# Branch prefetch hints placed inside the last second matmul of a ReGLU MLP kernel, and none on SyncE

## The chip, the cores and the metric

The kernel runs on one core of a Trainium2 chip. Times are device microseconds (us) of an execution. The profile's span, from the first to the last instruction, is about 1.8 us shorter than that time.

## The reference

```python
# x (16, 256, 512), w1 (512, 4096), w2 (2048, 512), all float32
h = x @ w1
gate, value = np.split(h, 2, axis=-1)
h = np.maximum(gate, 0) * value
return (h @ w2).astype(np.float32)
```

## The kernel before

The kernel has a fast way in float16, with fewer products per block than the plain method, and a general way for inputs whose sizes do not fit. While the last second matmul runs, the fast way judges statistics of the inputs and writes a flag. Every engine loads that flag into a register and branches (in the kernel before, 488 to 695 ns for the load and 45 to 496 ns for the branch). With the inputs used here the branch is always taken, over the whole body of the general way, to the end of the program.

```python
def tile_reglu_mlp_kernel(ctx, tc, x, w1, w2, out):
    ...                                             # cut
    with ExitStack() as fast:
        unfit = fast_way(fast, tc, x2, w1, w2, out2, flag)
    with tc.If(unfit > 0, label="general"):
        with ExitStack() as general:
            general_way(general, tc, x2, w1, w2, out2)
```

The fast way is written under a "manual schedule": each engine's instructions keep the order in which they were traced. The second matmul is a stream of 112 steps of four matmuls, and jobs are hung on its steps:

```python
    ctx.enter_context(tc.manual_schedule(engines={ENG.PE, ENG.DVE, ENG.Activation, ENG.Pool, ENG.SP}))
    ...                                             # cut
            job(18, lambda: verdict.append(judge()))
            job(46, lambda: count(verdict[0]))
            job(78, lambda: verdict.append(nc.values_load(flag[0:1, 0:1], ...)))      # cut
            job(84, lambda: tc.mark_branch_hint_location("general", "LikelyTaken", [ENG.PE, ENG.DVE, ENG.SP]))
            advance(stream, 112, jobs)
```

A branch prefetch hint is an instruction of its own, BRANCH_PREFETCH_HINT in the traces (50 ns on PE, 51 on VectorE and 56 on SyncE in the kernel before), that is marked for a later branch; what it does at that branch is what the runs below measure. The last job asks for it at step 84. But in the built program the hints of PE (TensorE), VectorE (DVE) and SyncE (SP) stand as the first instruction of each engine, about 300 us ahead of the branch. The last outputs go out as three 128 KB transfers, one after another, from SyncE, each behind the copy that made its tile.

## Time and profile before

| | before |
|---|---|
| time, median of the first 3 runs | 308.57 us (308.36 to 308.63) |
| span of the profile | 307.2 us |
| PE busy | 301.6 us, 98% |
| end of the last ScalarE copy | 303.45 us |
| last output: issue, landing | 303.48, 306.19 us |

From the page of the kernel before (busy us, share of the span, x instructions; then the chain that ended last, by engine):

```profile
PE 301.6 (98%) x1905; PEld 184.2 (60%) x1905; DVE 236.0 (77%) x388; ACT 176.3 (57%) x348; POOL 151.2 (49%) x189
...
q8 instruction: 16, 0.26, 0.4%
q14 instruction: 12, 0.10, 0.1%
...
PE 96%; DMA 2%; SPq 1%; issue 0%; ACT 0%
```

PE bounds the kernel. The two lines of queues (packets, MB, share) are the instruction fetches. q8 carries 16 KB packets and is put down to PE: it has 17 in the three runs where PE's branch took over 4 us (e1, e3, e9), 16 in all others with a branch and 15 without one (e11). q14 carries 8 KB packets and is put down to the other engines: it has one more where VectorE's hint does not act (13 in e5, 14 in e6).

The start of the chain in order of time (start, length, what), of the kernel before:

```profile
0.68 0.06 issue
0.74 0.06 SPq L785
0.80 0.06 issue
0.85 0.40 SPq L488
...
2.79 5.41 DMA x_A<-in_x_dram
```

L785 is SyncE's hint (all end-of-program and hint instructions bear that line). It stands between the start barrier and the first load of x, and a tile of x is what PE waits for until 8.2 us.

The branches, in the view of source line L42 (duration minimum/median/maximum in ns, then first and last start in us), of the kernel before:

```profile
L42 PEldq COMPARE_BRANCH  x1: 496/496/496, 301.9 to 301.9; - x1
L42 DVEq COMPARE_BRANCH  x1: 90/90/90, 302.2 to 302.2; - x1
L42 DVEq EVENT_SEMAPHORE  x1: 21/21/21, 302.8 to 302.8; - x1
L42 PEldq EVENT_SEMAPHORE  x1: 51/51/51, 303.1 to 303.1; - x1
...
L42 SPq COMPARE_BRANCH  x1: 68/68/68, 304.9 to 304.9; - x1
```

The event semaphore of each engine is the first instruction at the branch's target.

### The profile page before, as it was taken

What the parts mean: (1) busy time and instruction counts of PE and PEld (TensorE: products, weight loads), DVE (VectorE), ACT (ScalarE), POOL (GpSimd) and SP (SyncE); (2) the same over time, 40 slices, a digit from 0 to 9 for tenths busy, and PEclk for the clock granted to TensorE, in tenths of its full rate; (3) what the DMA queues carried; (4) which work ended last, traced back from release to release, by engine and by line L of the source; (5) the groups of instructions that cost most, each with busy time, mean ns of one, the idle gap of its engine ahead of it and who ended that gap; (6) DMA issues with size and microseconds to landing.
All of it is one profiled execution on the core that took longest, in us unless ns stands there. A gap on an engine that the chain in (4) does not pass through costs nothing.

```text
span 307.2 us, 5283 instructions
## 1 busy us (share of the span) xinstructions
PE 301.6 (98%) x1905; PEld 184.2 (60%) x1905; DVE 236.0 (77%) x388; ACT 176.3 (57%) x348; POOL 151.2 (49%) x189
## 2 busy tenths in 40 slices
PE   8999999999999999999999999999999999999994
PEld 7744444588844444478864444458884444447883
DVE  2579888899778888887538888888536888888851
ACT  2488896455865555537855555546866555553231
POOL 2389999800068999300029889700007988700000
PEclk9999999999999999999999999999999999999999
DMA  6985779965775270001354910000325110001132
GB/s 204 358 259 179 239 171 176 229 123 80 260 209 88 69 137 3 0 0 55 136 182 108 207 34 2 0 2 9 130 101 174 35 34 0 3 1 34 54 106 87
DMA packets 35836, 32.87 MB, mean 107 GB/s; under 512 B 14432, under 2 KB 31328, under 8 KB 35680
## 3 DMA queue, kind: packets, MB, share of 16 engines
q1 hardware_dynamic: 33536, 26.22, 28.3%
q0 software_dynamic: 2272, 6.29, 11.4%
q8 instruction: 16, 0.26, 0.4%
q14 instruction: 12, 0.10, 0.1%
HBM read 27.26 MB, written 12.58 MB: 130 GB/s over the span
## 4 chain that ended last, share of the span: by engine, by line
PE 96%; DMA 2%; SPq 1%; issue 0%; ACT 0%
PE Y L250 26%; PE X L250 17%; PE W L250 17%; PE Y L362 14%; PE W L362 9%; PE X L362 9%; DMA x_A<-in_x_dram 2%; PE X L325 1%; PE W L325 1%; PE Y L325 1%; PE Y L498 0%; PE X L498 0%; SPq L217 0%; SPq L488 0%; ACT o L405 0%
## 5 line engine op out<-in xcount | busy, mean ns | idle before, releaser
L250 PEld LDWEIGHTS <-w_T 128*128 128x128 f16 x496 | 48.3, 98 | 57.3 <-POOL w_T L232 1.1
L179 POOL TENSOR_TENSOR fold<-xh 128x1024 f32<-128x1024 f16 x16 | 30.3, 1894 | 94.6 <-DMA xh<-x 93.7
L250 PE MATMUL X<-x_A,w_B 128*128 128x512 f16 x248 | 73.8, 379 | 0.0
L250 PE MATMUL Y<-x_S,w_T 128*128 128x512 f16 x220 | 65.5, 379 | 0.0
L250 PEld LDWEIGHTS <-w_B 128*128 128x128 f16 x372 | 36.3, 98 | 42.1
L277 DVE SCALAR_TENSOR_TENSOR cc<-W,pu 128x512 f32<-128x512 f32 x62 | 42.9, 691 | 21.1 <-ACT pu L271 21.1
L257 ACT COPY Y<-X 128x512 f32<-128x512 f32 x62 | 35.4, 571 | 38.2 <-PE X L250 37.9
L271 ACT ACTIVATE pu<-Y 128x512 f32<-128x512 f32 x62 | 37.1, 598 | 33.9 <-PE Y L250 33.0
L182 POOL TENSOR_TENSOR fold<-fold 128x512 f32<-128x512 f32 (+2 forms) x96 | 51.8, 539 | 7.5
L362 PEld LDWEIGHTS <-w_stage 128*128 128x128 f16 x512 | 50.0, 98 | 5.9
L287 DVE SCALAR_TENSOR_TENSOR cc<-Y,pu 128x512 f32<-128x512 f32 x62 | 42.9, 691 | 6.7
L282 DVE SCALAR_TENSOR_TENSOR g<-X,cc 128x512 f16<-128x512 f32 x62 | 42.8, 691 | 2.3
L299 DVE SCALAR_TENSOR_TENSOR g<-Y,cc 128x512 f16<-128x512 f32 x62 | 42.2, 681 | 1.8 <-PE Y L250 1.8
L362 PEld LDWEIGHTS <-g 128*128 128x128 f16 x384 | 37.5, 98 | 8.2
L264 ACT ACTIVATE pu<-W 128x512 f32<-128x512 f32 x62 | 37.2, 600 | 0.8 <-PE W L250 0.6
L250 PE MATMUL W<-x_S,w_B 128*128 128x512 f16 x124 | 36.9, 379 | 0.0
L250 PE MATMUL W<-x_S,w_T 128*128 128x512 f16 x124 | 36.9, 379 | 0.0
L250 PE MATMUL Y<-x_A,w_T 128*128 128x512 f16 x124 | 36.9, 379 | 0.0
L362 PE MATMUL X<-w,g 128*128 128x256 f16 x256 | 31.9, 273 | 0.0
L394 DVE SCALAR_TENSOR_TENSOR o<-W,pu 128x256 f32<-128x256 f32 x16 | 6.8, 423 | 19.4 <-PE W L362 19.4
L169 DVE TENSOR_TENSOR w_stage<-g 128x1024 f16<-128x1024 f16 x32 | 21.4, 684 | 0.2
L232 POOL TENSOR_TENSOR w_T<-w_stage 128x512 f16<-128x512 f32 (+1 forms) x16 | 18.7, 1173 | 2.5 <-DMA w_stage<-in_w_dram 2.5
(100 smaller groups left out, 307.5 us busy)
## 6 DMA issues: line engine op xcount, KB each, us to landing
w_stage<-in_w_dram SPq DMA_DIRECT2D x14, 512.0 KB, 6.0
out_dram<-o SPq DMA_DIRECT2D x26, 256.0 KB, 2.1
x<-in_x_dram POOLq DMA_DIRECT2D x4, 1024.0 KB, 9.1
xh<-x SPq DMA_DIRECT2D x16, 256.0 KB, 3.0
w<-in_w_dram POOLq DMA_DIRECT2D x2, 1024.0 KB, 10.2
out_dram<-o SPq DMA_DIRECT2D x12, 128.0 KB, 1.7
w_stage<-in_w_dram SPq DMA_DIRECT2D x4, 256.0 KB, 5.4
x_S<-in_x_dram SPq DMA_DIRECT2D x4, 256.0 KB, 6.5
```

The costliest lines, as they stand in the source:

```text
L169: eng.tensor_tensor(o[n], o[i0], o[i1], op=op)
L179: nc.gpsimd.tensor_tensor(fold, t, t, op=MULT)
L182: nc.gpsimd.tensor_tensor(fold[:, :, :m], fold[:, :, :m], fold[:, :, m:2 * m], op=ADD)
L250: nc.tensor.matmul(ps, wop[wn][:, b, self.jb * P:(self.jb + 1) * P], self.xo[xn][:, b, :], start=fresh and b == 0, stop=b == 1, skip_group ...
L257: nc.scalar.copy(out=self.Y, in_=self.X)
L264: nc.scalar.activation(self.p5, self.W, COPY, scale=GS)
L271: nc.scalar.activation(self.u2, self.Y, COPY, scale=GS)
L277: nc.vector.scalar_tensor_tensor(out=self.c12, in0=self.W, scalar=GS, in1=self.u2, op0=MULT, op1=ADD)
L282: nc.vector.scalar_tensor_tensor(out=self.g[:, self.jb, :TH], in0=self.X, scalar=0.0, in1=self.c12, op0=MAX, op1=MULT)
L287: nc.vector.scalar_tensor_tensor(out=self.c22, in0=self.Y, scalar=GS, in1=self.p5, op0=MULT, op1=ADD)
L299: nc.vector.scalar_tensor_tensor(out=self.g[:, self.jb, TH:], in0=self.Y, scalar=0.0, in1=self.c22, op0=MAX, op1=MULT)
L362: nc.tensor.matmul(ps, self.op[an][:, i], vop[wn][:, i], start=name in ("P1", "P5") and i == 0, stop=i == NJ // 2 - 1, skip_group_check=True)
```

## The change

The intent is that the hint stands where it was asked for, near the branch, and that SyncE, whose program is short, has none. To pin the hint, the manual order is left, the hint is marked with a dependency on the engine's last traced instruction, and the manual order is entered again.

```diff
+    order = ctx.enter_context(ExitStack())
+    def in_order():
+        order.enter_context(tc.manual_schedule(engines={ENG.PE, ENG.DVE, ENG.Activation, ENG.Pool, ENG.SP}))
+    in_order()
...
+    def hint_here():
+        order.close()
+        traced = nc.cur_bb.bb.instructions
+        n = len(traced)
+        tc.mark_branch_hint_location("general", "LikelyTaken", [ENG.PE, ENG.DVE])
+        for i in nc.cur_bb.bb.instructions[n:]:
+            last = next(x for x in reversed(traced[:n]) if x.engine == i.engine and "Tile" not in type(x).__name__)
+            tc.add_manual_dep(i, last.name, ..., reason="the hint stays where it was traced")   # cut
+        in_order()
...
-            job(84, lambda: tc.mark_branch_hint_location("general", "LikelyTaken", [ENG.PE, ENG.DVE, ENG.SP]))
+            job(40, hint_here)
```

More of the change, by code (lines that the diff above doesn't have):

```diff
@@ L113, in fast_way @@
     NB = 2 * TH // P
-    ctx.enter_context(tc.manual_schedule(engines={ENG.PE, ENG.DVE, ENG.Activation, ENG.Pool, ENG.SP}))
+    order = ctx.enter_context(ExitStack())
+    def in_order():
+        order.enter_context(tc.manual_schedule(engines={ENG.PE, ENG.DVE, ENG.Activation, ENG.Pool, ENG.SP}))
+    in_order()
     wpool = ctx.enter_context(tc.tile_pool(name="wpool", bufs=1))
@@ L645, in judge @@
         return fit
+    def hint_here():
[5 more added lines that the diff above has]
+            last = next(x for x in reversed(traced[:n]) if x.engine == i.engine and "Tile" not in type(x).__name__)
+            tc.add_manual_dep(i, last.name, mybir.DependencyInfo(mybir.DependencyClass.NoSync, mybir.DependencyReason.DATA),
+                              reason="the hint stays where it was traced")
+        in_order()
     def count(fit):
```

## The prediction

> **What bounds the kernel now.** TensorE. The page gives PE 301.6 us busy of a 307.2 us span (98%), clock 0.999; the chain that ended last is 96% PE. The rest are two ends. At the start the chain runs through SyncE: its branch hint (0.74 to 0.80 us), its DMA issues from 0.85 us, then an x tile's landing until 8.2 us, which releases transposes. At the end, in the timeline: last matmul about 303.05, last ScalarE copy until 303.45, last output DMA issue until 304.8, its landing about 306.3, closing barrier until 307.2.
>
> **What the change does**, by the order of instructions on each engine:
> - SyncE loses its hint (56 ns, in the chain at 0.74 us).
> - PE and VectorE lose theirs at the start (50 and 51 ns, about 0.8 us). Neither is in the chain.
> - PE gets its hint in the last second matmul, just before product P5 of pair 1 (about 286.9 us); VectorE just before the flag's comparison (about 288.7 us).
> - A side effect: one VectorE sum (S1 of pair 2, 0.68 us) moves from just before the flag to inside the judgement, after its first comparison (284.2 us). ScalarE and GpSimd keep their order.
>
> **What it is worth.** The intent is a cheaper taken branch over the general body. The view of that source line shows the branches: PE's starts at 301.9 and takes 0.50 us, its next instruction is at 303.1; VectorE's starts at 302.2 (0.09 us), next at 302.8; SyncE's at 304.9 (0.07 us), next at 305.1. [...] But both reach the final barrier by about 303.2, while SyncE waits for the last output until 306.3: 3 us of slack. So a faster branch is worth no time. SyncE's branch also lies before the wait for the landing, and its gap of 0.1 us shows no fetch wait.
>
> On the critical path remain:
> - start: -0.06 us (without SyncE's hint every x load issues earlier).
> - PE's hint in a stream of matmuls 0.109 us apart: 0 to +0.05 us[...].
> - the moved sum delays the sums of pair 1 by 0.68 us. S1 of pair 1 would end at about 286.2, needed at 286.85; S2 at 286.9, needed at 287.7; the others have over 1 us. No new PE wait.
>
> Sum: about -0.03 us, below the spread of the three runs (308.36 to 308.63).
>
> **Predicted: 308.5 us, 308.1 to 308.9 in 8 of 10. Faster by over 2%: 0.01; within 2%: 0.98; slower by over 2%: 0.01.**
>
> **What would show each step.** First x issue at about 0.79 instead of 0.85 us; hints of about 50 ns at 287 and 289 us; PE's matmuls there still 0.109 us apart; PE's branch perhaps down from 0.50 to 0.1 us and its closing drain earlier, with the last landing and the end of the span unmoved; no PE wait for a sum at 286 to 290 us.
>
> **What would make it wrong.** [...] If the hint at the first instruction had disturbed fetching for the whole run, PE would gain, but at 98% busy there is little to gain. If the moved sum waits for PE, up to 1 us could be added.

## The result

| | before | after |
|---|---|---|
| time, median of 6 runs each | 308.54 us (308.28 to 308.84) | 308.24 us (307.99 to 308.39) |
| span of the profile | 307.2 us | 306.4 us |
| PE's branch | 496 ns | 496 ns |
| VectorE: end of branch to first instruction at its target | 0.54 us | 3.11 us |
| last output, issue to landing | 2.71 us | 2.60 us |

Ratio 0.9989, 95% interval 0.9976 to 1.0002. The change is within 2%, and a gain is not clear of noise by this pair alone.

The start of the chain after the change:

```profile
0.73 0.13 issue
0.86 0.28 DVE warm L149
1.15 0.05 issue
1.19 2.74 PE Y L153 x24
```

SyncE's first x issue, after:

```profile
0.74 0.87 SPq L493 DMA_DIRECT2D x_A<-in_x_dram  x2
```

It moved from 0.85 to 0.74 us, by 0.11 us: the hint and the gap behind it. In this run x landed early enough that PE never waited for it, and the chain begins at VectorE's memset instead. That memset too is earlier, from 0.95 to 0.86 us, because VectorE's hint is gone from in front of it.

The branches after the change:

```profile
L42 PEldq COMPARE_BRANCH  x1: 496/496/496, 301.3 to 301.3; - x1
L42 DVEq COMPARE_BRANCH  x1: 90/90/90, 301.6 to 301.6; - x1
L42 PEldq EVENT_SEMAPHORE  x1: 51/51/51, 302.5 to 302.5; - x1
...
L42 SPq COMPARE_BRANCH  x1: 53/53/53, 303.2 to 303.2; - x1
L42 DVEq EVENT_SEMAPHORE  x1: 21/21/21, 304.8 to 304.8; - x1
```

PE's branch is what it was. VectorE's has become 2.6 us worse, with a hint 15 us ahead of it. The instruction fetches after the change:

```profile
q8 instruction: 16, 0.26, 0.4%
q14 instruction: 14, 0.11, 0.1%
```

Of the two packets that q14 has more, only one belongs to VectorE's branch. The other, at 96.6 us, goes with SyncE: it stands in every trace without a hint on SyncE and is missing in the two with one (before and e12).

Matching PE's 1905 matmuls one by one, PE is 0.62 to 0.64 us earlier than before from 11 us on, and this lead changes by no more than 40 ns from one matmul to the next up to the end. So PE's late hint and the moved VectorE sum cost PE nothing, and all of the lead arises at the start. How far it is a property of the change, and not of that one run's loads, the experiments must tell.

### The profile page after: what moved, and what is told of

Read it like the earlier page. It is cut to its first block, busy times and chain, and to the rows that moved or that the text cites. A ratio compares the mean times of both kernels' runs of the same rounds, so it can differ in the third digit from the quotient of the medians.

```text
span 306.4 us, 5282 instructions
## 1 busy us (share of the span) xinstructions
PE 301.2 (98%) x1905; PEld 184.6 (60%) x1905; DVE 235.7 (77%) x388; ACT 176.4 (58%) x348; POOL 151.3 (49%) x189
## 3 DMA queue, kind: packets, MB, share of 16 engines
q0 software_dynamic: 2272, 6.29, 11.4%
## 4 chain that ended last, share of the span: by engine, by line
PE 98%; ACT 0%; DVE 0%; issue 0%
PE Y L255 26%; PE X L255 17%; PE W L255 17%; PE Y L367 14%; PE X L367 9%; PE W L367 9%; PE X L330 1%; PE Y L153 1%; PE W L330 1%; PE Y L503 1%; PE Y L330 1%; PE X L503 1%; PE Y L520 0%; PE Y L159 0%; PE Y L154 0%; ACT o L410 0%
```

## The experiments

Two questions came from the traces. Why did VectorE's branch lose 2.6 us with a hint closer to it, and does that matter? And where do the 0.3 us come from? Theory A: an engine keeps its hint until the branch, however early it was given, but the late hint on VectorE came too late for a fetch to be started. The rival B: hints do nothing, and 0.54 against 3.11 us is chance.

The first table gives, for every run, where the hints executed and what the branches did. The "fetch" is the engine's last instruction block fetch ahead of the branch, worked out from the times of the trace's instruction packets: 268 to 270 us on VectorE and 297.8 to 299.1 us on PE, except where noted.

| run | PE hint at | VectorE hint at | PE branch | VectorE gap | last output, issue to landing |
|---|---|---|---|---|---|
| before | 0.8 us | 0.8 us | 0.50 us | 0.54 us | 2.71 us |
| after | 285.2 | 286.5 | 0.50 | 3.11 | 2.60 |
| e1_no_hints | none | none | 4.48 | 3.03 | 3.94 |
| e2_no_sp | 0.8 | 0.8 | 0.50 | 0.54 | 2.46 |
| e3_moved_sum | none | none | 4.46 | 3.01 | 3.30 |
| e4_mid2 | 234.1 | 235.6 | 0.41 | 0.54 | 2.23 |
| e5_before_fetch | 264.2 | 265.7 | 0.41 | 0.54 | 2.35 |
| e6_after_fetch | 278.8 | 281.2 | 0.50 | 3.18 | 2.35 |
| e7_pe_just_ahead | 296.3 | 295.9 | 0.50 | 2.95 | 2.78 |
| e8_pe_just_behind | 298.0 (fetch at 299.9) | 296.0 | 0.66 | 3.07 | 2.98 |
| e9_pe_behind | 299.2 | 300.6 | 4.33 | 3.07 | 3.15 |
| e10_e8_again | 298.0 (fetch at 299.9) | 296.0 | 0.68 | 3.04 | 2.66 |
| e11_no_branch | no branch | no branch | none | none | 1.69 |
| e12_sp_hints_x8 | 0.8 | 0.8 | 0.50 | 0.54 | 2.62 |

The second table gives the times. Kernels of one group ran on the same chip in the same rounds.

| run | median us (range) | before, same rounds | ratio (95%) |
|---|---|---|---|
| e1_no_hints | 308.43 (307.52 to 310.36) | 308.28 | 0.9992 (0.9974 to 1.0010) |
| e2_no_sp | 308.20 (308.07 to 309.02) | 308.28 | 0.9991 (0.9978 to 1.0004) |
| e3_moved_sum | 308.93 (307.82 to 309.37) | 308.28 | 1.0008 (0.9992 to 1.0024) |
| e4_mid2 | 308.07 (307.82 to 308.51) | 308.28 | 0.9988 (0.9975 to 1.0000) |
| e5_before_fetch | 308.33, one run | 308.42 | - |
| e6_after_fetch | 308.06 (307.75 to 308.41) | 308.42 | 0.9996 (0.9979 to 1.0014) |
| e7_pe_just_ahead | 308.37 (307.82 to 308.57) | 308.42 | 0.9996 (0.9980 to 1.0012) |
| e8_pe_just_behind | 308.97 (308.65 to 309.08) | 308.42 | 1.0020 (1.0005 to 1.0035) |
| e9_pe_behind | 308.06 (307.63 to 308.84) | 308.45 | 0.9981 (0.9963 to 1.0000) |
| e10_e8_again | 308.88 (308.55 to 309.16) | 308.45 | 1.0010 (0.9989 to 1.0032) |
| e11_no_branch | 307.76 (307.44 to 308.17) | 308.45 | 0.9973 (0.9956 to 0.9991) |
| e12_sp_hints_x8 | 311.15 (310.64 to 311.46) | 308.45 | 1.0078 (1.0060 to 1.0096) |

All gave the right result. The kernel before itself ranged from 307.81 to 309.70 us in the last group, so differences of 0.3 us need care.

### e1_no_hints: no hint anywhere

```diff
-            job(84, lambda: tc.mark_branch_hint_location("general", "LikelyTaken", [ENG.PE, ENG.DVE, ENG.SP]))
```

> Kernel before with no hint on any engine. Theory A (the hint at the first instruction was kept until the branch, the late VectorE hint came too late to start a fetch): VectorE's gap after its branch is about 3.1 us as in the changed kernel, against 0.54 us before; if PE's hint also did something, PE's next instruction after its branch comes 1 us or more later than before's 1.2 us. Rival B (hints do nothing, 0.54 against 3.11 us is chance): VectorE's gap 0.5 us or anything. Time: if PE's branch also stalls by 3 us or more, PE ends after the last output's landing (2.7 us after the last ScalarE copy) and the time is 308.5 to 310 us; if only VectorE's stalls, 308.2 to 308.6 us. The start is as in the changed kernel: first x issue at about 0.8 us.

The branches without hints:

```profile
L42 PEldq COMPARE_BRANCH  x1: 4476/4476/4476, 302.1 to 302.1; - x1
L42 DVEq COMPARE_BRANCH  x1: 72/72/72, 302.4 to 302.4; - x1
L42 DVEq EVENT_SEMAPHORE  x1: 21/21/21, 305.5 to 305.5; - x1
L42 PEldq EVENT_SEMAPHORE  x1: 51/51/51, 306.6 to 306.6; - x1
```

Rival B falls. The hint at the first instruction, 301 us ahead of the branch, had worked all along on both engines: it spares PE about 4 us and VectorE 2.5 us at the branch. And VectorE's gap in the changed kernel is that of no hint at all. Yet PE was not the last engine even here. The last output landed at 307.62 us and PE drained at 306.77. The time did not settle what the miss costs: the six runs spread over 2.8 us.

### e2_no_sp: only SyncE's hint taken away

```diff
-..., [ENG.PE, ENG.DVE, ENG.SP]))
+..., [ENG.PE, ENG.DVE]))
```

> Kernel before, PE and VectorE hints at the first instruction kept, SyncE's hint left out. Theory A: VectorE's gap after its branch 0.54 us as before, PE as before. My account of the start: SyncE's first x issue 0.06 us earlier; time lower than before by 0.06 us. Rival C (the whole gain of 0.3 us comes through SyncE's hint): time lower by 0.3 us and PE's early lead of 0.2 to 0.64 us at 7.5 to 11 us seen again.

The first x issue came at 0.74 us, as after the change, and the branches are those of the kernel before. The ratio, 0.9991, is about that of the whole change (0.9989), but its interval includes both 0.06 and 0.3 us, so rival C was not excluded by the time. PE was 0.32 us behind the kernel before in this profile at 12 us, not ahead: the early lead is not seen again, and the profiles of single runs differ by more than the effect.

### e3_moved_sum: the changed kernel without its hints

```diff
-        tc.mark_branch_hint_location("general", "LikelyTaken", [ENG.PE, ENG.DVE])
```

> Changed kernel with its two late hints taken out: what remains is the moved VectorE sum and no hint anywhere. If the moved sum costs nothing: time equal to that of the kernel without hints within 0.15 us, PE's matmuls 0.109 us apart from 282 us on, no wait for a sum. If the late hints cost PE time, this is faster than the changed kernel by up to 0.05 us. If the late PE hint helps PE's branch, PE's next instruction after its branch comes 1 us or more later than the changed kernel's 1.2 us after the branch starts.

This keeps the one VectorE sum that leaving and re-entering the manual order had moved. From 11.4 us on, PE's matmuls keep a constant distance to the kernel before's, so the moved sum costs nothing. PE's branch took 4.46 us, so the late hint of the changed kernel does act on PE. The median is 0.50 us above that of e1, but e1's spread is too wide for the comparison that was expected.

### e4_mid2: both hints at 234 us, in no changed order

```diff
-            job(40, hint_here)
+                if (s, n, jb) == (NS - 1, "P1", 2):      # in the last first matmul
+                    hint_here()
```

> Hints of PE and VectorE put at the second block of the last first matmul's stage (about 235 us), SyncE none, and no moved sum. Theory A: about 90 program lines of VectorE lie between hint and branch and the fetch is started in time: VectorE's gap after its branch 0.5 us. Rival B: anything. Time within 0.1 us of the kernel without SyncE's hint, as VectorE and PE still have slack.

VectorE's gap is 0.54 us again, as expected. Here and in e5 to e10, except that instruction, PE and VectorE have the order of the kernel before; only the hints stand elsewhere. This kernel has both branches served and no SyncE hint. Its median is 0.2 us below the kernel before and its interval just reaches 1. It is 0.13 us below e2, where 0.1 us at most was expected; their ranges overlap.

### e5_before_fetch and e6_after_fetch: around VectorE's last fetch

In the traces VectorE's instruction blocks are fetched about every 127 instructions (in the changed kernel's trace 66, 193, 318 and 446 of its instructions start ahead of the fetches at 40.6, 108.0, 187.9 and 268.6 us), and the last fetch before its branch is at 268 to 270 us. Theory A2 sharpens A: a hint acts if it stands ahead of that fetch.

```diff
-            job(40, hint_here)
+                if (s, n, jb) == (NS - 1, "P1", 12):     # e5
+                    hint_here()
```

```diff
-            job(40, hint_here)
+            job(12, hint_here)                           # e6
```

> Hints of PE and VectorE at block 12 of the last first matmul's stage; on VectorE about 8 instructions ahead of the fetch that the traces show at 268.6 to 269.6 us, the last one there before the branch. Theory A2 (a hint acts only when it stands ahead of the engine's last block fetch before the branch, and then turns that fetch to the branch's target): VectorE's gap 0.54 us, PE's branch 0.4 to 0.5 us. Rival D (a hint needs many instructions of distance, 100 or more): VectorE's gap 3.1 us.

> Both hints early in the last second matmul, with no sum moved; on VectorE about 14 instructions behind that last fetch and still about 40 ahead of the branch, over 25 us in time. Theory A2: VectorE's gap 3.1 us as in the changed kernel, PE's branch 0.5 us (PE has fetches left). Rival E (the changed kernel's hint was only too near the branch in time or was disturbed by the moved sum): VectorE's gap 0.54 us. Time within 0.15 us of the kernel before without SyncE's hint, as VectorE still ends before the last landing.

VectorE's lines of e5, then of e6 (the hint is from the view of its own line):

```profile
L803 DVEq BRANCH_PREFETCH_HINT  x1: 51/51/51, 265.7 to 265.7; - x1
...
L42 DVEq COMPARE_BRANCH  x1: 90/90/90, 301.9 to 301.9; - x1
L42 DVEq EVENT_SEMAPHORE  x1: 21/21/21, 302.5 to 302.5; - x1
```

```profile
L802 DVEq BRANCH_PREFETCH_HINT  x1: 51/51/51, 281.2 to 281.2; - x1
...
L42 DVEq COMPARE_BRANCH  x1: 90/90/90, 301.4 to 301.4; - x1
L42 DVEq EVENT_SEMAPHORE  x1: 21/21/21, 304.7 to 304.7; - x1
```

A hint at 265.7 us, 3 us ahead of the fetch, works; a hint at 281.2 us, still 20 us ahead of the branch, does nothing. A2 is confirmed for VectorE, and rivals D and E fall: neither the distance in time nor the moved sum is what failed. The changed kernel's hint at 286.5 us stands on the wrong side of 268.6 us. That the last fetch is turned to the target fits the counts (q14 has 13 packets in e4 and 14 in e1 without hints, PE's q8 has 16 and 17), but which block a packet held is not in the trace; that part is argued.

### e7_pe_just_ahead and e8_pe_just_behind: around PE's last fetch

```diff
-            job(40, hint_here)
+            job(88, hint_here)                           # e7;  job(100, ...) in e8
```

> Hints near the end of the last second matmul: PE's about 97 rows before its branch, about 30 rows ahead of PE's last fetch (298.0 to 298.8 us). Theory A2: PE's branch 0.5 us and time equal to that of the changed kernel within 0.2 us; VectorE's gap 3.1 us. Rival D: PE's branch about 4.5 us.

> The same with PE's hint about 49 rows before its branch, about 15 rows behind PE's last fetch. Theory A2: PE's branch 4.4 us as with no hint at all, PE last at the closing barrier, the barrier opened about 0.7 us after the last landing instead of at it: time 0.5 to 0.8 us above e7_pe_just_ahead. If 0.5 us here too, theory A2 is wrong for PE.

e7 came out as expected. e8 did not: PE's hint ran at 297.99 us, so it was not behind the fetch, and the fetch itself came at 299.9 us in place of 298 us. The branch took 0.66 us, not 4.4. So e8 did not test what it was meant to. But it was 0.6 us slower than e7 all the same, with its lowest run above e7's highest, for a reason that my expectation does not hold.

### e9_pe_behind and e10_e8_again

```diff
-            job(40, hint_here)
+            job(104, hint_here)                          # e9;  job(100, ...) again in e10
```

> PE's hint about 33 rows before its branch. In e8 the hint ran at 297.99 us and the fetch came after it (299.9 us, branch 0.66 us), so e8 did not test what it was meant to; this hint is about 16 rows later and should come after the fetch at 298.0 to 298.8 us. Theory A2: fetch at its usual 298 us, PE's branch about 4.4 us as without a hint, time 0.4 to 0.8 us over the kernel before. If PE's branch is below 1 us again, a hint acts for PE even behind its last regular fetch, and A2 is wrong for PE.

> e8 once more, because it was 0.6 us slow though its branch took 0.66 us. Theory F (the end is set by PE's 16 KB instruction block, fetched right after the branch on one of the 16 DMA engines that carry the last outputs: in the traces the last output lands 1.0 to 1.5 us after that block's end, and the block took 1.6 us in e8 against 1.0 to 1.4 elsewhere): the last output lands about 1.05 us or more after that block's end again, and the block takes 1.5 us or more if the slowness is systematic. Time 308.7 to 309.1 us again if it is; else 308.0 to 308.5 us and e8's slowness was chance.

In e9 the hint ran at 299.2 us, behind the fetch at 297.8 us, and PE's branch took 4.33 us, as with no hint:

```profile
L42 PEldq COMPARE_BRANCH  x1: 4332/4332/4332, 301.1 to 301.1; - x1
...
L42 PEldq EVENT_SEMAPHORE  x1: 51/51/51, 305.5 to 305.5; - x1
```

So A2 holds for PE too. That the hint was merely too near the branch in time does not explain it: it ran 1.9 us ahead, and the branch was only 0.13 to 0.15 us shorter than with no hint (4.46 and 4.48 us). Its forecast of the time failed: e9 was not slower than the kernel before (0.9981). PE drained at 305.62 us and the last output landed at 305.82 us, so PE was again not last, by 0.2 us.

e10 came out high again (308.88 us). Its mean is 0.70 us above e9's of the same rounds, with a standard error of 0.23, but its interval against the kernel before includes 1; so e8's slowness is probably systematic. Theory F's reason for it failed as it stood: PE's block after the branch took 0.93 us here, not 1.5 us or more. (The profile is of the fastest of e10's four runs.) F's rule held: the last packet of the outputs ended 1.05 us after that block's end, and the last output landed 1.5 us after it. In e10 the block was not longer, but it began late, 1.82 us after the start of PE's branch; in the other nine traces with a working hint on PE that was 1.25 to 1.69 us. It ended 3.07 us after that start in e8 and 2.75 in e10, against 2.24 to 2.69 in the other eight. Why a hint so close to the usual time of the fetch does this stays open.

### e11_no_branch: what the whole branch costs

```diff
-    with tc.If(unfit > 0, label="general"):
-        with ExitStack() as general:
-            general_way(general, tc, x2, w1, w2, out2)
...
-            job(78, ...)                                 # the reading of the flag
-            job(84, ...)                                 # the hints
```

> Kernel before without the general way, its branch, the reading of the flag and the hints; right for these inputs only, a measurement and no candidate. Prices the whole branch. Theory F: no instruction block is fetched in the last 4 us, the last outputs land about 1.7 to 2.0 us after their issue instead of 2.4 to 3.0, and the time from PE's end to the end of the span falls from about 4.0 us to about 3.2; time 0.5 to 1.0 us below the kernel before. My prediction's picture (a branch with a good hint costs nothing in time): time within 0.2 us of the kernel without SyncE's hint.

This is no candidate, since it drops the fallback. The DMA in the tail of the kernel before, of the changed kernel and of this one, from 301 us on (queues: packets, MB, share; issues: count, KB, median us from issue to landing):

```profile
q8 instruction: 1, 0.02, 1.0%
q14 instruction: 1, 0.01, 0.3%
issues: line engine op xcount, KB each, median us to landing
out_dram<-o SPq DMA_DIRECT2D x3, 128.0 KB, 2.7
```

```profile
q8 instruction: 1, 0.02, 0.8%
q14 instruction: 2, 0.02, 0.6%
issues: line engine op xcount, KB each, median us to landing
out_dram<-o SPq DMA_DIRECT2D x3, 128.0 KB, 2.6
```

```profile
q1 hardware_dynamic: 432, 0.39, 14.5%
issues: line engine op xcount, KB each, median us to landing
out_dram<-o SPq DMA_DIRECT2D x3, 128.0 KB, 1.7
```

Without a branch no instruction block is fetched during the last outputs, and they land in 1.7 us. With it, one more 16 KB block of PE is fetched once PE is at the branch's target, even when the hint worked; it takes 0.9 to 1.6 us in those traces, and runs while the last two outputs are under way. The last output then lands 2.2 to 3.0 us after its issue. In the changed kernel's packets all but two pieces of the last outputs are done by 304.5 us, and two last packets of 4 bytes follow at 304.7 and 305.0 us, after the 16 KB block ended at 303.96. Without a branch the three outputs' packets come in three compact groups with no straggler. In the kernel before the delay has another form: the last piece of the second output ends at 305.15 us, the second output has landed at 305.63 us, and all pieces of the third end only then, at 305.69 to 305.84 us. The packets of all traces make the link firmer. In the ten with a working hint on PE, the last output packet ended 1.04 to 1.06 us (after, e4, e5, e8, e10) or 1.35 to 1.40 us (before, e2, e6, e7, e12) after the end of PE's block, although that end itself came 2.24 to 3.07 us after the start of PE's branch. The 8 KB block in the same stretch keeps no such distance (1.2 to 2.1 us). So the end of the kernel follows PE's block. That a piece queues behind it on one DMA engine is argued from these times; the trace does not name the engine.

The whole time fell by 0.8 us by the ratio. Some of that is SyncE's missing hint, as this kernel has none. The reading of the flag is gone too, but its absence gained PE nothing: PE is 0.27 us ahead of the kernel before at 11.5 us and still at its last matmul. From the end of the last ScalarE copy to the end of the span the profile has 2.67 us, against 3.71 in the kernel before.

### e12_sp_hints_x8: eight hints on SyncE

```diff
+ the same mark made 7 times more, for [ENG.SP] alone
```

> Kernel before with eight hints in place of one on SyncE at its start, PE and VectorE as before. In the traces one hint moves SyncE's first x issue from 0.74 to 0.85 us, 0.11 us. So the first x issue at about 1.6 us. If the start passes this through to the end: time 0.6 to 0.8 us above the kernel before. If PE's warm-up matmuls or the DMA queues hide it: less than 0.3 us, and then SyncE's hint cannot be what the change gained.

SyncE's first x issue:

```profile
1.35 0.88 SPq L488 DMA_DIRECT2D x_A<-in_x_dram  x2
```

The later hints take only 31 ns each, so the loads moved by about 0.5 us against the kernel before, not 0.75. The time rose by 2.7 us, far more than expected, but only part of that is the start. The mean span of its six runs is 307.2 us, against 306.8 us for the kernel before of the same rounds: 0.4 us. The other 2.1 us lie outside the span: the time exceeds the span by 3.9 us here and by 1.8 us in all other kernels. In this trace two packets of q14 follow after the span's end; that SyncE's longer program fetches one block more there is argued, not shown. By these means 0.4 of the 0.5 us of delay reached the end. But the standard error of that difference is 0.23 us, and e2's profile was 0.34 us behind the kernel before with no hint on SyncE at all. So it is suggested, not shown, that most of a delay of SyncE's first load reaches the end.

## Why the prediction was right or wrong

**The time: right.** 308.24 us was measured, 308.5 predicted, in a range of 308.1 to 308.9. The class, within 2%, was right as well. One part of this is luck: VectorE's branch got worse, against the prediction, and only a slack that was not planned hid it (below).

**"start: -0.06 us": the mechanism was right and the size too small.** The term counted the hint's 56 ns and left out the gap behind it. The first x issue moved by 0.11 us, and e12 suggests that such a shift mostly reaches the end. It was also wrong that neither of the other two hints is in the chain: in the changed kernel's profile the chain begins at VectorE's memset, 0.09 us earlier without the hint. Which of the two starts the chain depends on when x lands in that run. Both together make about 0.1 us, an estimate from these two shifts. The rest of the 0.30 us between the medians is not shown to be real. The ratios of the kernels with no SyncE hint and a PE hint well ahead of the fetch (the change, e2, e4, e6, e7) are 0.9988 to 0.9996, all below 1 and none clear of it.

**"PE's hint ... 0 to +0.05 us": right.** PE's matmuls show no step at 285 us: they start 0.109 to 0.110 us apart there. The term itself was my estimate. One fetch was late: 286.2 us in place of 284.2 to 285.5 in the other traces.

**"No new PE wait" from the moved sum: right**, in the changed kernel and in e3.

**"PE's branch perhaps down from 0.50 to 0.1 us": wrong.** It stayed at 496 ns. I had read the 0.50 us as a possible fetch wait, an estimate that no trace had shown. The hint at the first instruction had already shortened the branch; with no hint it takes 4.48 us (e1). The intent of the change fails at the same place: an early hint is not lost (0.50 us with the hint at 0.8 us).

**VectorE's branch: missed.** The prediction expected a gain or nothing. The gap rose from 0.54 to 3.11 us, because the hint stands behind VectorE's last block fetch (286.5 against 268.6 us). So "3 us of slack" no longer holds after the change: VectorE drains at 304.91 us and the last output lands at 305.46, a slack of 0.55 us. It was just enough, and this was luck of placement, not foresight.

**"A faster branch is worth no time": half right.** No engine's branch was last in any of these traces, even with a 4.5 us miss, since SyncE waits for the last output longer (until 307.62 us in e1, where PE drained at 306.77). But the branch is not free. Its fetch accompanies the last outputs on their way, and without any branch they land in 1.7 us in place of 2.2 or more. The prediction treated the landing as fixed, but it follows the end of PE's block after the branch (1.05 or 1.4 us to the last packet), so the time at which PE reaches the target may matter. What a given shift of PE's branch is worth was not measured. Whether a PE miss costs time stays unsettled: in the profiles the stretch from the last copy to the end of the span is 4.1 to 4.9 us with a miss and 3.2 to 4.0 us without, while e9's times show no loss and e3's mean is 0.68 us (standard error 0.26) above that of e4 of the same rounds, though not clear of the kernel before.

When no hint acts, VectorE's next instruction came 2.95 to 3.18 us after its branch, against 0.54 us, and PE's branch took 4.33 to 4.48 us, against 0.41 to 0.68 us. ScalarE and GpSimd never had a hint, and SyncE had none after the change, yet their next instruction came 0.13, 0.43 and 0.14 us after the branch; why they waited no longer is not in the trace. The branch itself took 45 to 90 ns on VectorE, ScalarE, GpSimd and SyncE.

Of the kernels tried, e4_mid2 is the version to keep by its traces: both branches served, no SyncE hint, no sum moved, and the shortest landing of those with a branch. By its times it is not shown to beat the change.

## What to carry to other kernels

In these runs a prefetch hint acted only where it stood ahead of the engine's last instruction block fetch before the branch: on VectorE at 265.7 us but not at 281.2, on PE at 298.0 us but not at 299.2. Being earlier than that, even at the first instruction, did no harm at the branch (0.50 us on PE, 0.54 on VectorE); being later made it useless (4.33 and 3.18 us). Look at the first instruction at the branch's target to see whether a hint worked, and at what the closing barrier waits for to see whether it matters. Look also for instruction fetches while the last outputs are on their way: here the last packet ended 1.05 or 1.4 us behind PE's block. And a hint in front of the first load delayed that load's issue by 0.11 us.
